# Modulation weights in tiles of their own, multiplied in bursts, in a one-layer diffusion backbone

## The chip, the cores and the metric

The kernel runs on one core of a Trainium2 chip. The time is device time in microseconds (us) of one execution. The kernel before took 2011.56, 2011.78 and 2003.14 us in three runs, a median of 2011.56 us.

The engines named below are TensorE (PE, with PEld for its weight loads), VectorE (DVE), ScalarE (ACT), GpSimd (POOL) and SyncE (SP, which issues the DMAs that this change touches). Each executes its instructions in the order in which they stand in its program, and that order is fixed when the kernel is built.

## The reference, cut to what matters

One trunk layer over 128 context tokens and 256 latent tokens of width 2048. A modulation vector is made of the condition by a product with `w_ada` (2048 x 12288 fp32, 100.7 MB), and is split in six:

```python
mod_ctx = (silu(c_ctx) @ w_ada + b_ada)      # for the context tokens
mod_lat = (silu(c) @ w_ada + b_ada)          # for the latent tokens
shift1, scale1, gate1, shift2, scale2, gate2 = split(mod, 6)
h = rmsnorm(x, pre1) * (1 + scale1) + shift1
proj = h @ w_in                              # gated DeltaNet heads, mLSTM heads, gates
x = x + gate1 * rmsnorm(concat(delta_heads, mlstm_heads) @ w_out, post1)
h = rmsnorm(x, pre2) * (1 + scale2) + shift2
x = x + gate2 * rmsnorm(relu(h @ w1) ** 2 @ w2, post2)
```

The final states of the two kinds of heads are outputs too. All is fp32; `w_in` has 7216 columns, `w1` and `w2` 8192 columns and rows.

## The kernel before, in words

**Large products.** `gemm` (L342) takes a weight matrix by chunks of 256 rows x 512 columns (512 KB). `wchunk` (L321) loads a chunk into a tile `raw` by one DMA on SP's queue (L328), rounds it to `whi` on ScalarE (L332), and takes the rest `wlo = raw - whi` on VectorE (L333). TensorE then makes three products to a pair of tiles (L356 to L358 where the weights are the stationary side and 384 tokens stream, L360 to L362 where the tokens are stationary and 512 weight columns stream): 24 matmuls to a chunk in the first form, 18 in the second.

**The modulation.** `ada_steps` (L172) multiplies `w_ada` by the two condition vectors, spread over 32 columns (`scz`). Each matmul has 32 output rows and goes to one of four column groups of TensorE (`ps[32 * j:32 * j + 32]`), so that four of them stand side by side. In phase 1 a call has two units (the shift1 and the scale1 columns of the same 128 or 256 features); later it has four units of 256 columns. `ada_vec` (L209) does the same sum on VectorE instead, one `scalar_tensor_tensor` (L220) to a row tile and vector, for part of the last two vectors.

**Who decides when.** Both are generators. The list `S.todo` holds them, and after each chunk `gemm` calls `fill` (L235), which hands out steps by a rate: 2.0 steps to a chunk in phase 1, 1.3 in the delta stage, 0.9 in the output projection, 0.3 in the FFN. `drain` (L250) finishes a unit where its result is needed next. A step is one tile of 512 KB: its DMAs (two of 256 KB in phase 1, one later), and its 8 matmuls of 256 columns (or 16 of 128), or in `ada_vec` four VectorE operations. The order of the finished program on each engine is a scheduler's, by these calls and by `high_priority`.

**Buffers.** All loads, of weights and of modulation weights, share one ring: tag `raw` in the pool `wp`, `nraw=5` tiles of 512 KB. `whi` and `wlo` have two tiles each.

**Stages.** In the profiled execution phase 1 (`phase1`, L395: nine pieces of input features, each first modulated by `build_hT`, L288, then multiplied by columns of `w_in`) and the mLSTM heads take roughly the first 320 us, the DeltaNet heads and their output gates go to about 790 us, `mid` (the output projection and the second norm) to about 930 us, and `ffn` and `final` take the rest.

Of the kernel before, what the change touches and what calls it, by code (L numbers as in the profile page):

```python
# [12 lines left out]
F32 = mybir.dt.float32  # L13
# [8 lines left out]
P = 128  # L22
# [148 lines left out]
def ada_steps(S, units, n):  # L171

    nc, c = S.nc, S.c
    nu = len(units)
    npar = 4 // nu
    kn = 1024 // (nu * n)
    ps = S.pa.tile([P, 512], F32, tag="a", name="ps_ada")
    for k in range(0, NK, kn):  # L180
        raw = S.wp.tile([P, kn, nu * n], F32, tag="raw", name="raw_ada", bufs=S.nraw)
        runs = [(0, nu)] if nu == 4 else [(u, u + 1) for u in range(nu)]
        for u, e in runs:
            o = units[u][0] * D + units[u][1]
            nc.sync.dma_start(raw[:, :, u * n:e * n], S.A.w_ada[0, k * P:(k + kn) * P, o:o + (e - u) * n]
                              .rearrange("(k p) n -> p k n", p=P))
        for kk in range(kn):
            for u in range(nu):
                j = u * npar + (k + kk) % npar
                nc.tensor.matmul(ps[32 * j:32 * j + 32, 0:n], lhsT=c.scz[:, k + kk, :],  # L190
                                 rhs=raw[:, kk, u * n:u * n + n], start=k + kk < npar, stop=k + kk >= NK - npar)
        yield
# [11 lines left out]
def ada_vec(S, sec, c0):  # L204

    nc, c = S.nc, S.c
    while S.av is None:
        yield
    acc = S.av.tile([P, 2, 512], F32, tag="adav", name="adav", bufs=1)  # L209
    for kt in range(NK):  # L210
        if kt % 2 == 0:
            raw = S.wp.tile([P, 2, 512], F32, tag="raw", name="raw_av", bufs=S.nraw)
            nc.sync.dma_start(raw, S.A.w_ada[0, kt * P:(kt + 2) * P, sec * D + c0:sec * D + c0 + 512]
                              .rearrange("(k p) n -> p k n", p=P))
        for v in range(2):
            w = c.scz[:, kt, v:v + 1]
            if kt == 0:
                nc.vector.tensor_scalar(acc[:, v, :], raw[:, 0, :], w, None, op0=ALU.mult)
            else:
                nc.vector.scalar_tensor_tensor(acc[:, v, :], in0=raw[:, kt % 2, :], scalar=w, in1=acc[:, v, :],  # L220
                                               op0=ALU.mult, op1=ALU.add)
        if kt % 2:
            yield
# [11 lines left out]
def fill(S, n=None):  # L235

    if n is None:
        S.credit += S.rate
        n = int(S.credit)
        S.credit -= n  # L240
    while n > 0 and S.todo:
        try:
            next(S.todo[0])
            n -= 1
        except StopIteration:
            S.todo.pop(0)
            n -= 1
# [1043 lines left out]
```

## Time and profile before

| what | value |
|---|---|
| timed runs | 2011.56, 2011.78, 2003.14 us |
| the profiled execution | 2004.86 us |
| its span | 2003.1 us |
| PE busy | 1944.5 us, 97% |
| DVE busy | 1166.2 us, 58% |
| ACT busy | 711.1 us, 35% |
| modulation matmuls L190 | 1216 records, 100.6 us busy |
| moved by DMA | 337.25 MB, mean 168 GB/s |

A row of the page's table of groups gives busy time, the mean of one instruction, the idle time of its engine just before it and what ended that. A row of a timeline gives the start in the span, the time, the engine, the line, and in brackets the idle time ahead of it and its releaser. TensorE's rows overlap, since its matmuls are pipelined: the time from one start to the next is what a matmul costs there, not its own length.

### The profile page before, as it was taken

The page shows a single profiled execution, that of the slowest core. Times are in us where ns is not written, and L with a number is a line of the kernel's source. Part 1 is how long each engine was busy: PE and PEld are TensorE (multiplying, and loading weights), DVE is VectorE, ACT ScalarE, POOL GpSimd, SP SyncE. Part 2 cuts the span into 40 slices and gives each one's busy share as a digit, 9 for nine tenths or more (in the row PEclk, how much of TensorE's full clock was granted, in tenths as well). Part 3 has the DMA queues.
Part 4 walks back from the last instruction along what each step waited for, and adds up shares of the span by engine and source line. Part 5 has one row for each costly group of instructions (what it writes and reads, how often), then busy time and mean ns, then how long its engine had stood idle before and what let it go on. Part 6 is the DMA issues. An engine that isn't in the chain of part 4 may idle for free.

```text
span 2003.1 us, 28836 instructions
## 1 busy us (share of the span) xinstructions
PE 1944.5 (97%) x11332; PEld 1673.4 (84%) x11332; DVE 1166.2 (58%) x2144; ACT 711.1 (35%) x1125; POOL 122.8 (6%) x125
## 2 busy tenths in 40 slices
PE   5999997999999999998999999999999999999997
PEld 4677886788888777787998898998989989989886
DVE  3766874668878766767455455556543443343445
ACT  5222243544344334335433342332332423323322
POOL 2000000010000000000100010000000100000002
PEclk9999998999999999998999999999999999999999
DMA  9988438776576566762454554545544344444452
GB/s 271 297 263 261 127 117 167 171 198 192 162 200 188 154 189 201 269 220 64 127 178 158 158 160 147 172 162 158 163 136 130 122 135 126 126 128 127 131 172 105
DMA packets 232356, 337.25 MB, mean 168 GB/s; under 512 B 46272, under 2 KB 115584, under 8 KB 231196
## 3 DMA queue, kind: packets, MB, share of 16 engines
q1 hardware_dynamic: 214120, 333.15, 55.1%
q10 hardware_dynamic: 17620, 2.11, 0.7%
q8 instruction: 89, 1.46, 0.3%
q14 instruction: 47, 0.39, 0.1%
q0 software_dynamic: 480, 0.15, 0.0%
HBM read 326.80 MB, written 8.56 MB: 167 GB/s over the span
## 4 chain that ended last, share of the span: by engine, by line
PE 89%; DMA 5%; DVE 4%; ACT 1%; issue 1%; POOL 0%; SPq 0%; ACTq 0%; DVEq 0%; POOLq 0%
PE ps_g L356 13%; PE ps_g L358 13%; PE ps_g L357 12%; PE ps_dn L360 8%; PE ps_dn L362 8%; PE ps_dn L361 8%; PE ps_g L360 5%; PE ps_g L362 5%; PE ps_g L361 5%; PE ps_ada L190 4%; DMA raw<-w_in 2%; DVE wlo L333 1%; PE ps_o L1027 1%; DMA raw_av<-w_ada 1%; PE ps_num L689 1%
## 5 line engine op out<-in xcount | busy, mean ns | idle before, releaser
L333 DVE TENSOR_TENSOR wlo<-raw,whi 128x1024 fp32r<-128x1024 f32 (+1 forms) x402 | 487.2, 1212 | 568.9 <-ACT whi L332 567.3
L332 ACT CAST whi<-raw 128x1024 fp32r<-128x1024 f32 (+1 forms) x402 | 417.5, 1039 | 1012.3 <-PE ps_g L357 386.8
L356 PE MATMUL ps_g<-h,whi 128*128 128x384 f32 x1536 | 522.8, 340 | 0.6 <-DVE cv L737 0.6
L358 PE MATMUL ps_g<-h,wlo 128*128 128x384 f32 x1536 | 516.3, 337 | 2.1 <-DVE wlo L333 2.1
L357 PE MATMUL ps_g<-h,whi 128*128 128x384 f32 x1536 | 517.0, 337 | 0.0
L356 PEld LDWEIGHTS ps_g<-h,whi 128*128 128x128 f32 x1536 | 288.9, 188 | 20.7 <-issue 18.7
L362 PE MATMUL ps_dn<-wlo,ah 128*128 128x512 f32 x756 | 294.5, 390 | 1.2 <-DVE wlo L333 1.2
L360 PE MATMUL ps_dn<-whi,al 128*128 128x512 f32 x756 | 294.8, 390 | 0.0
L361 PE MATMUL ps_dn<-whi,ah 128*128 128x512 f32 x756 | 294.5, 390 | 0.0
L358 PEld LDWEIGHTS ps_g<-h,wlo 128*128 128x128 f32 x1536 | 288.6, 188 | 5.1 <-DVE wlo L333 3.6
L357 PEld LDWEIGHTS ps_g<-h,whi 128*128 128x128 f32 x1536 | 288.9, 188 | 1.2 <-issue 0.7
L362 PEld LDWEIGHTS ps_dn<-wlo,ah 128*128 128x128 f32 x756 | 141.9, 188 | 31.5 <-DVE wlo L333 2.0
L360 PEld LDWEIGHTS ps_dn<-whi,al 128*128 128x128 f32 x756 | 141.9, 188 | 31.0 <-issue 1.6
L361 PEld LDWEIGHTS ps_dn<-whi,ah 128*128 128x128 f32 x756 | 141.9, 188 | 29.0
L220 DVE SCALAR_TENSOR_TENSOR adav<-raw_av,scz,adav 128x512 f32<-128x512 f32 x180 | 130.4, 773 | 12.3 <-DMA raw_av<-w_ada 12.3
L1148 POOL TENSOR_TENSOR rl<-rl 128x384 f32<-128x384 f32 x64 | 68.0, 1070 | 876.2 <-ACT ah L1147 876.0
L360 PE MATMUL ps_g<-whi,h 128*128 128x512 f32 x288 | 119.1, 413 | 1.3 <-ACT whi L332 1.2
L361 PE MATMUL ps_g<-whi,h 128*128 128x512 f32 x288 | 115.2, 400 | 0.0
L362 PE MATMUL ps_g<-wlo,h 128*128 128x512 f32 x288 | 114.2, 400 | 0.2 <-DVE wlo L333 0.2
L190 PE MATMUL ps_ada<-raw_ada,scz 128*32 128x256 f32 (+1 forms) x1216 | 100.6, 387 | 4.0 <-DMA raw_ada<-w_ada 2.6
L360 PEld LDWEIGHTS ps_g<-whi,h 128*128 128x128 f32 x288 | 54.5, 189 | 24.2 <-issue 11.7
L190 PEld LDWEIGHTS ps_ada<-raw_ada,scz 128*32 128x32 f32 x1216 | 33.9, 113 | 46.4 <-issue 27.2
(400 smaller groups left out, 1895.5 us busy)
## 6 DMA issues: line engine op xcount, KB each, us to landing
raw<-w_ffn SPq DMA_DIRECT2D x256, 512.0 KB, 3.8
raw_ada<-w_ada SPq DMA_DIRECT2D x80, 512.0 KB, 4.8
raw<-w_in SPq DMA_DIRECT2D x74, 512.0 KB, 4.7
raw_ada<-w_ada SPq DMA_DIRECT2D x128, 256.0 KB, 4.5
raw_av<-w_ada SPq DMA_DIRECT2D x48, 512.0 KB, 4.3
raw<-w_in SPq DMA_DIRECT2D x76, 256.0 KB, 3.1
raw<-w_out SPq DMA_DIRECT2D x32, 512.0 KB, 4.5
x<-x_sample SPq DMA_DIRECT2D x2, 1024.0 KB, 10.3
```

The lines of the kernel that those rows point to most:

```text
L190: nc.tensor.matmul(ps[32 * j:32 * j + 32, 0:n], lhsT=c.scz[:, k + kk, :], rhs=raw[:, kk, u * n:u * n + n], start=k + kk < npar, stop=k + k ...
L220: nc.vector.scalar_tensor_tensor(acc[:, v, :], in0=raw[:, kt % 2, :], scalar=w, in1=acc[:, v, :], op0=ALU.mult, op1=ALU.add)
L332: nc.scalar.copy(hi, raw)
L333: nc.vector.tensor_tensor(lo, raw, hi.bitcast(F32), op=ALU.subtract)
L356: nc.tensor.matmul(o, lhsT=hi[:, kk, w], rhs=al, start=st, stop=False)
L357: nc.tensor.matmul(o, lhsT=hi[:, kk, w], rhs=ah, start=False, stop=False)
L358: nc.tensor.matmul(o, lhsT=lo[:, kk, w], rhs=ah, start=False, stop=sp)
L360: nc.tensor.matmul(o, lhsT=al[:, w], rhs=hi[:, kk, :], start=st, stop=False)
L361: nc.tensor.matmul(o, lhsT=ah[:, w], rhs=hi[:, kk, :], start=False, stop=False)
L362: nc.tensor.matmul(o, lhsT=ah[:, w], rhs=lo[:, kk, :], start=False, stop=sp)
L689: nc.tensor.matmul(o, lhsT=l, rhs=r, start=n == 0, stop=n == len(ops) - 1)
L1148: nc.gpsimd.tensor_tensor(rl, rl, rl, op=ALU.mult)
```

## The change: what it does

- `ada_steps` no longer takes tiles of the ring `raw`. In phase 1 it has two tiles of 1 MB, `rawa` (in `wp`) and `rawb` (in `p1`), and after phase 1 `rawa` alone, each with one buffer.
- A step is now a burst: all loads of the burst are issued (in phase 1 2 MB by four DMAs, later 1 MB by one DMA), and then all its matmuls, the last tile and its last row first, so that the first matmul reads what was loaded last. The flags that open and close the sum are counted per column group. A burst has 32 matmuls of 128 columns in the first two units of phase 1, 16 of 256 columns in the others, and 8 of 256 later.
- `yield` gives what the step cost (4 for two tiles, 2 for one), and `fill` takes that from the credit, which may fall below nothing; `drain` ends with a credit of 0.
- `ada_vec` takes 1 MB (four row tiles) into `rawa` by one DMA, and issues the next load right behind the last operation that reads the tile.
- The ring `raw` has 3 tiles (`nraw=3`).

The changed lines stand 9 to 15 lines lower: L190 is L199, the loads L185 are L191, L213 is L222, L220 is L233, L328 is L342, L333 is L347, L360 to L362 are L374 to L376.

```diff
@@ -172,24 +172,33 @@
 
 
 
+
+
     nc, c = S.nc, S.c
     nu = len(units)
     npar = 4 // nu
-    kn = 1024 // (nu * n)
+    kn = 2048 // (nu * n)
     ps = S.pa.tile([P, 512], F32, tag="a", name="ps_ada")
-    for k in range(0, NK, kn):
-        raw = S.wp.tile([P, kn, nu * n], F32, tag="raw", name="raw_ada", bufs=S.nraw)
-        runs = [(0, nu)] if nu == 4 else [(u, u + 1) for u in range(nu)]
-        for u, e in runs:
-            o = units[u][0] * D + units[u][1]
-            nc.sync.dma_start(raw[:, :, u * n:e * n], S.A.w_ada[0, k * P:(k + kn) * P, o:o + (e - u) * n]
-                              .rearrange("(k p) n -> p k n", p=P))
-        for kk in range(kn):
-            for u in range(nu):
-                j = u * npar + (k + kk) % npar
-                nc.tensor.matmul(ps[32 * j:32 * j + 32, 0:n], lhsT=c.scz[:, k + kk, :],
-                                 rhs=raw[:, kk, u * n:u * n + n], start=k + kk < npar, stop=k + kk >= NK - npar)
-        yield
+    runs = [(0, nu)] if nu == 4 else [(u, u + 1) for u in range(nu)]
+    done = [0] * 4
+    kb = kn * len(S.araw)
+    for k0 in range(0, NK, kb):
+        raws = []
+        for (pool, tag), k in zip(S.araw, range(k0, NK, kn)):
+            raw = pool.tile([P, kn, nu * n], F32, tag=tag, name="raw_ada", bufs=1)
+            for u, e in runs:
+                o = units[u][0] * D + units[u][1]
+                nc.sync.dma_start(raw[:, :, u * n:e * n], S.A.w_ada[0, k * P:(k + kn) * P, o:o + (e - u) * n]
+                                  .rearrange("(k p) n -> p k n", p=P))
+            raws.append((k, raw))
+        for k, raw in raws[::-1]:
+            for kk in range(kn)[::-1]:
+                for u in range(nu)[::-1]:
+                    j = u * npar + (k + kk) % npar
+                    done[j] += 1
+                    nc.tensor.matmul(ps[32 * j:32 * j + 32, 0:n], lhsT=c.scz[:, k + kk, :],
+                                     rhs=raw[:, kk, u * n:u * n + n], start=done[j] == 1, stop=done[j] == NK // npar)
+        yield 2 * len(raws)
     t = ada_cols(S, ps, n)
     m = n // P
     if npar == 1:
@@ -205,22 +214,28 @@
 
     nc, c = S.nc, S.c
     while S.av is None:
-        yield
+        yield 1
     acc = S.av.tile([P, 2, 512], F32, tag="adav", name="adav", bufs=1)
+
+    def load(kt):
+        raw = S.wp.tile([P, 4, 512], F32, tag="rawa", name="raw_av", bufs=1)
+        nc.sync.dma_start(raw, S.A.w_ada[0, kt * P:(kt + 4) * P, sec * D + c0:sec * D + c0 + 512]
+                          .rearrange("(k p) n -> p k n", p=P))
+        return raw
+    raw = load(0)
+    yield 1
     for kt in range(NK):
-        if kt % 2 == 0:
-            raw = S.wp.tile([P, 2, 512], F32, tag="raw", name="raw_av", bufs=S.nraw)
-            nc.sync.dma_start(raw, S.A.w_ada[0, kt * P:(kt + 2) * P, sec * D + c0:sec * D + c0 + 512]
-                              .rearrange("(k p) n -> p k n", p=P))
         for v in range(2):
             w = c.scz[:, kt, v:v + 1]
             if kt == 0:
                 nc.vector.tensor_scalar(acc[:, v, :], raw[:, 0, :], w, None, op0=ALU.mult)
             else:
-                nc.vector.scalar_tensor_tensor(acc[:, v, :], in0=raw[:, kt % 2, :], scalar=w, in1=acc[:, v, :],
+                nc.vector.scalar_tensor_tensor(acc[:, v, :], in0=raw[:, kt % 4, :], scalar=w, in1=acc[:, v, :],
                                                op0=ALU.mult, op1=ALU.add)
+        if kt % 4 == 3 and kt < NK - 1:
+            raw = load(kt + 1)
         if kt % 2:
-            yield
+            yield 1
     ps = S.pa.tile([P, 512], F32, tag="a", name="ps_av")
     for j in range(4):
         nc.tensor.matmul(ps[32 * j:32 * j + 32, 0:256], lhsT=c.ones[:, 0:32], rhs=acc[:, j % 2, 256 * (j // 2):][:, 0:256],
@@ -234,22 +249,21 @@
 
 def fill(S, n=None):
 
-    if n is None:
-        S.credit += S.rate
-        n = int(S.credit)
-        S.credit -= n
-    while n > 0 and S.todo:
+
+    S.credit += S.rate if n is None else n
+    while S.credit >= 1 and S.todo:
         try:
-            next(S.todo[0])
-            n -= 1
+            S.credit -= next(S.todo[0])
         except StopIteration:
             S.todo.pop(0)
-            n -= 1
+            S.credit -= 1
 
 
 def drain(S, left):
     while len(S.todo) > left:
-        fill(S, 1)
+        S.credit = 1
+        fill(S, 0)
+    S.credit = 0.0
 
 
 def ada_later(S, sec, nvec=0):
@@ -263,7 +277,7 @@
 
 def gate_step(S, i):
     gate_rows(S, i)
-    yield
+    yield 1
 
 
 def gate_rows(S, i):
@@ -405,6 +419,7 @@
     NP = len(pieces)
     S.todo = [ada_steps(S, [(0, P * k), (1, P * k)], P * kn) for k, kn in pieces]
     S.rate = 2.0
+    S.araw = [(S.wp, "rawa"), (p1, "rawb")]
 
     for p, (k0, kn) in enumerate(pieces):
         if p == 0:
@@ -1207,7 +1222,7 @@
 def body(tc, A, O):
     with ExitStack() as ctx:
         nc = tc.nc
-        S = SimpleNamespace(nc=nc, tc=tc, A=A, O=O, todo=[], credit=0.0, rate=1.7, nraw=5, av=None)
+        S = SimpleNamespace(nc=nc, tc=tc, A=A, O=O, todo=[], credit=0.0, rate=1.7, nraw=3, av=None)
         ent = ctx.enter_context
         sub = lambda st, nm, bufs=1: st.enter_context(tc.tile_pool(name=nm, bufs=bufs, reuse_waits="tile"))
         S.cp = ent(tc.tile_pool(name="cp", bufs=1))
@@ -1236,6 +1251,7 @@
                 S.ml = sub(ms, "ml", 2)
                 for h in range(HB):
                     mlstm_head(S, h)
+            S.araw = [(S.wp, "rawa")]
             S.da = sub(mx, "da", 2)
             S.dl = sub(mx, "dl", 2)
             S.de = sub(mx, "de", 2)
```

Three places of the order of the instructions follow. A row names the line, the operation, what it writes and reads, and the size; "x4" is four alike in a row.

SP in phase 1, at the first units of 256 columns, before (`raw_ada` are modulation weights, `raw` weights of `w_in`):

```order
L328 DMA raw<-w_in 128x2x512
L185 DMA raw_ada<-w_ada 128x2x256 x4
L328 DMA raw<-w_in 128x2x512
L185 DMA raw_ada<-w_ada 128x2x256 x4
L328 DMA raw<-w_in 128x2x512
L185 DMA raw_ada<-w_ada 128x2x256 x4
```

The same place now, with the semaphores for which an instruction waits (PE is a wait for matmuls, DVE for the operations that end the use of a `raw` tile, DMAHW for an earlier DMA):

```order
L342 DMA raw<-w_in 128x2x512 [waits DMAHW6_49,DVE_49]
L342 DMA raw<-w_in 128x2x512 [waits DMAHW7_49,DVE_49]
L191 DMA raw_ada<-w_ada 128x4x256 [waits DMAHW4_49,DMAHW3_49,PE_49]
L191 DMA raw_ada<-w_ada 128x4x256 [waits DMAHW1_49,DMAHW2_49,DMAHW0_49,PE_49]
L191 DMA raw_ada<-w_ada 128x4x256 x2
L342 DMA raw<-w_in 128x2x512 [waits DVE_49]
L342 DMA raw<-w_in 128x2x512 [waits DMAHW5_49,DVE_49]
```

Four loads of 512 KB now stand together, the first of them waits for TensorE, and the loads of `w_in` stand behind them.

TensorE in phase 1, in the products with tokens stationary, before (`ps_ada` is the modulation, `ps_g` the product with `w_in`):

```order
L190 MATMUL ps_ada<-raw_ada,scz 32x256 x4
L360 MATMUL ps_g<-whi,h_171 128x512
L361 MATMUL ps_g<-whi,h_170 128x512
L362 MATMUL ps_g<-wlo,h_170 128x512
L165 MATMUL ps_col<-ident,modrow 128x128 x2
L360 MATMUL ps_g<-whi,h_171 128x512
```

And now:

```order
L199 MATMUL ps_ada<-raw_ada,scz 32x256 x16
L376 MATMUL ps_g<-wlo,h_170 128x512
L374 MATMUL ps_g<-whi,h_171 128x512
L375 MATMUL ps_g<-whi,h_170 128x512
L165 MATMUL ps_col<-ident,modrow 128x128 x2
L376 MATMUL ps_g<-wlo,h_170 128x512
```

Runs of 1 to 8 modulation matmuls became runs of 16; over the whole program the number of such runs falls from 119 to 67.

VectorE at the end of `mid`, where the second norm is made, before (L1113 adds the residual, L310 makes the matrix `diag` for which TensorE waits):

```order
L1113 SCALAR_TENSOR_TENSOR x_1_8124<-x_1_8124,r1r,xr_8129 128x1024
L1081 TENSOR_TENSOR x_2_8125<-ps_g,gp_1_8127 128x512
L1108 TENSOR_REDUCE s_9144<-ssm 128x1
L1118 TENSOR_REDUCE s_9154<-ss_9123 128x1
L282 TENSOR_SCALAR r1v<-s_9144 128x1
L282 TENSOR_SCALAR r20v<-s_9154 128x1
L1113 SCALAR_TENSOR_TENSOR x_2_8125<-x_2_8125,r1r,xr_8130 128x1024 x2
L310 TENSOR_SCALAR diag<-ident,r20r 128x128
```

And now:

```order
L1128 SCALAR_TENSOR_TENSOR x_1_7976<-x_1_7976,r1r,xr_7981 128x1024
L1123 TENSOR_REDUCE s_8955<-ssm 128x1
L1133 TENSOR_REDUCE s_8965<-ss_8934 128x1
L233 SCALAR_TENSOR_TENSOR adav<-raw_av,scz,adav 128x512
L296 TENSOR_SCALAR r1v<-s_8955 128x1
L296 TENSOR_SCALAR r20v<-s_8965 128x1
L233 SCALAR_TENSOR_TENSOR adav<-raw_av,scz,adav 128x512
L1128 SCALAR_TENSOR_TENSOR x_2_7977<-x_2_7977,r1r,xr_7982 128x1024 x2
L324 TENSOR_SCALAR diag<-ident,r20r 128x128
L1133 TENSOR_REDUCE s_8973<-ss_8934 128x1
L233 SCALAR_TENSOR_TENSOR adav<-raw_av,scz,adav 128x512
L296 TENSOR_SCALAR r21v<-s_8973 128x1
```

Operations of `ada_vec` (`adav`) now stand among the steps of the norm, where there was none.

## Rows read from the trace of the kernel before

**Rows 1.** The page's first part: busy us, share of the span, instructions.
```profile
PE 1944.5 (97%) x11332; PEld 1673.4 (84%) x11332; DVE 1166.2 (58%) x2144; ACT 711.1 (35%) x1125; POOL 122.8 (6%) x125
```

**Rows 2.** Windows: stretch, length, busy PE, PEld, DVE, ACT, POOL, PEclk, DMA share, GB/s.
```profile
0.00:320.00 320.00, 298.61 (x1853) 233.33 (x1854) 212.01 (x440) 104.60 (x146) 14.44 (x27) 0.98 0.72 219
320.00:790.00 470.00, 454.99 (x3466) 370.19 (x3466) 328.27 (x949) 204.32 (x470) 21.20 (x16) 0.99 0.66 181
```

**Rows 3.** Windows of the same stretches, modulation matmuls L190 alone: PE, PEld.
```profile
0.00:320.00 320.00, 44.14 (x600) 17.69 (x600) 0.98 0.72 219
320.00:790.00 470.00, 55.85 (x608) 16.05 (x608) 0.99 0.66 181
```

**Rows 4.** Waits of PE: what waited, for what, us in total, times, longest.
```profile
PE ps_hT L295 <- DVE s L1118: 7.2, 1, 7.2
...
PE ps_ada L190 <- DMA raw_ada<-w_ada: 2.6, 1, 2.6
```

**Rows 5.** Timeline of PE around two runs of modulation matmuls in phase 1.
```profile
157.71 0.39 PE L361 MATMUL ps_g<-whi,h 128*128 128x512 f32 x1
157.94 0.39 PE L362 MATMUL ps_g<-wlo,h 128*128 128x512 f32 x1
158.25 1.07 PE L190 MATMUL ps_ada<-raw_ada,scz 128*32 128x256 f32 x16
159.25 0.50 PE L360 MATMUL ps_g<-whi,h 128*128 128x512 f32 x1
159.59 0.40 PE L361 MATMUL ps_g<-whi,h 128*128 128x512 f32 x1
...
38.37 0.40 PE L361 MATMUL ps_g<-whi,h 128*128 128x512 f32 x1
38.69 0.64 PE L190 MATMUL ps_ada<-raw_ada,scz 128*32 128x256 f32 x8
39.26 0.50 PE L362 MATMUL ps_g<-wlo,h 128*128 128x512 f32 x1
39.60 0.40 PE L360 MATMUL ps_g<-whi,h 128*128 128x512 f32 x1
```

**Rows 6.** DMA issues, 205 to 260 us: count, KB each, median us to landing.
```profile
raw<-w_in SPq DMA_DIRECT2D x13, 512.0 KB, 3.7
```

**Rows 7.** DMA issues of the whole span.
```profile
raw_ada<-w_ada SPq DMA_DIRECT2D x80, 512.0 KB, 4.8
...
gp<-gpd SPq DMA_DIRECT2D x2, 1024.0 KB, 8.0
```

**Rows 8.** Windows, columns as in rows 2: a light, a dense and a long stretch.
```profile
205.00:260.00 55.00, 55.00 (x275) 48.55 (x275) 46.26 (x72) 15.79 (x19) 0.00 (x0) 1.00 0.42 121
60.00:80.00 20.00, 19.32 (x130) 12.90 (x129) 16.62 (x35) 6.17 (x10) 0.00 (x0) 1.00 0.98 321
60.00:200.00 140.00, 139.09 (x910) 102.86 (x909) 96.79 (x173) 33.07 (x41) 0.00 (x0) 1.00 0.85 272
```

**Rows 9.** Timeline of PE near the start, around the second unit of modulation.
```profile
27.48 2.77 PE L190 MATMUL ps_ada<-raw_ada,scz 128*32 128x128 f32 x42 [1.31 <-DVE modcol L167]
30.18 0.59 PE L435 MATMUL ps_gates<-h,wgh 128*96 128x384 f32 x2
```

**Rows 10.** Windows around the second norm.
```profile
914.00:916.00 2.00, 0.00 (x0) 0.00 (x0) 1.00 (x6) 1.15 (x2) 0.70 (x2) 0.56 0.98 363
924.00:926.00 2.00, 2.00 (x15) 2.00 (x15) 1.89 (x5) 0.60 (x2) 0.00 (x0) 0.88 0.00 0
```

**Rows 11.** Timeline of DVE, then PE, at the end of the second norm.
```profile
918.27 0.28 DVE L310 TENSOR_SCALAR diag<-ident,r20r 128x128 f32<-128x128 f32 x1
...
918.61 0.80 PE L295 MATMUL ps_hT<-diag,x 128*128 128x128 f32 x2 [7.22 <-DVE s L1118]
```

**Rows 12.** Timeline of DVE in the FFN, one chunk with modulation work.
```profile
1147.04 1.23 DVE L333 TENSOR_TENSOR wlo<-raw,whi 128x1024 fp32r<-128x1024 f32 x1 [2.94 <-ACT whi L332]
1148.18 2.73 DVE L220 SCALAR_TENSOR_TENSOR adav<-raw_av,scz,adav 128x512 f32<-128x512 f32 x4
1151.20 1.23 DVE L333 TENSOR_TENSOR wlo<-raw,whi 128x1024 fp32r<-128x1024 f32 x1 [0.29 <-ACT whi L332]
```

## The prediction, made before the changed kernel ran

> **What bounds the kernel now.** I read the page's first part first, then windows by stage, the waits of TensorE, the windows of the modulation matmuls alone, and last timelines around single runs of them. TensorE is busy 97% of the span and the next engine 58% [rows 1]. In phase 1 and the delta stage it is busy 298.6 of 320 and 455.0 of 470 us [rows 2], so what it spends on the modulation, 44.1 and 55.9 us [rows 3], lies on the path, and a wait of TensorE put there lies on it too. The whole span has one wait of it for a modulation load, 2.6 us [rows 4]: the shared ring of five tiles lets these loads run ahead. The longest wait near the change is 7.2 us before the second norm's transposes [rows 4]. The change touches three things: the number of runs of modulation matmuls, when their loads may start, and where VectorE's share stands.
>
> **Fewer runs: -15.5 us.** A run costs more than its matmuls, because TensorE changes from full to 32-column work and back. Around a run of 8 matmuls (16 records) the starts go from 157.94 to 159.59, 1.65 us [rows 5]; five matmuls before it are 0.23 apart, of which two lie in this stretch (the one at 157.94 and the one at 159.25), so the run costs 1.65 - 0.46 = 1.19. A run of 4 costs 39.60 - 38.37 less two such, 1.23 - 0.46 = 0.77 [rows 5]. The difference gives 0.42 for four matmuls, 0.107 each, and leaves 0.77 - 0.43 = 0.34 us fixed to a run. By this rule (half for 128 columns) the 119 runs of before cost about 102 us, and the trace has 44.1 + 55.9 = 100 [rows 3], so the rule holds over the whole. Now there are 67 runs (order of the program): 52 x 0.34 = 17.7 us less. Before's first four runs stood in TensorE's idle start, where saving them is worth nothing, about 2.2 us: -15.5. If only the runs of 4 in the dense parts pay in full it may be -12; if the longer weight loads at a change (0.50 against 0.39 a matmul [rows 5]) are more than I count, -18.
>
> **The loads now wait for the burst before them.** Each tile has one buffer. By the order, the first load of a burst waits on SP for the last matmul of the burst before; nothing is loaded ahead of that. So each burst starts no sooner than one whole load after the last. How long is that? A lone load of 512 KB lands 3.7 us after its issue [rows 6], in a stretch with 121 GB/s [rows 8]. A dense stretch of 20 us moves 321 GB/s at a DMA share of 0.98 [rows 8], so the bytes take 1.6 us and 2.1 are fixed. 2 MB: 2.1 + 2.097/0.321 = 2.1 + 6.5 = 8.6 us. 1 MB: 2.1 + 3.3 = 5.4; the rows of 1 MB show 8.0 [rows 7], but those are broadcast reads.
> Against that stands the work between two bursts in TensorE's order. In phase 1 I counted the matmuls between bursts and took 0.2285 us for one of 512 columns and 0.1735 for one of 384 (pitch in long runs): between two bursts stand for instance 31 products and two transposes, 7.4 us. The 14 gaps behind the first full burst are 7.3, 5.9, 8.7, 6.8, 7.8, 7.5, 7.7, 8.5, 7.5, 7.5, 8.2, 7.3, 7.7 and 8.1 us, the sum of what 8.6 exceeds them by is 14 us. Take +14; with 7.0 us for a load it is 1, with 9.8 (the 272 GB/s of the long stretch [rows 8]: 2.1 + 7.7) 31. In the delta stage the 40 bursts have gaps of 4.7 to 22 us, eight of them of 5.0 and about ten more up to 5.7, where one chunk (24 x 0.1735 = 4.2 us) stands between. With 5.4 the sum is 4, with 5.7 8: take +6; at 5.0 it is 0.6, at 6.0 13.
> The weight loads behind the waiting instruction on SP are late too: by TensorE's time between bursts at most two chunks, and those of the ring's 3 tiles cover about two chunks of 4.1 us. I cost this at nothing, since whi and wlo of the next chunk are made ahead; if the cover is gone, `whi` waits 1 us in each of the 14 bursts, and that is in the upper end. Three tiles where nothing else is loaded: a lone load of 3.7 us within a chunk of 4.16 leaves two chunks of lead, nothing.
>
> A rule bears on the load. The Trainium skill ("DMA: Bandwidth & Descriptors", "Anatomy of one DMA") gives a DMA about 2.0 us fixed, and the rest by 436 GB/s. That makes an estimate of 3.2 us for 512 KB, where the trace has 3.7 [rows 6], and 6.8 for 2 MB, at which the waits of phase 1 would be about 1 us. The trace's rates are 321 over 20 us [rows 8] and 363 in 2 us [rows 10], and the sum goes by the first, which holds for longer than one load.
>
> **The start: +1 us.** Before, the second unit's matmuls stand ahead of the gates' product, 2.77 us of modulation until 30.18 [rows 9], and TensorE was at work through a time in which it now waits for the gate weights: now its first unit is one burst of 32, and the second comes after the first products. The clock may fall in such a wait; at the second norm 7.2 us of idle time bring it to 0.56 of full, and it is still at 0.88 some 6 us after the restart [rows 10], which is what it could cost here (up to 4 us). The 2 us of taking the second unit's matmuls off the start go the other way. Range -2 to +4, I take +1.
>
> **The second norm: +3 us.** Here VectorE is a chain of single steps, TensorE idles 7.2 us for it [rows 11]. In the order now, `adav` operations stand in it: two before the first `diag`, two before the second, and more behind. Each takes 0.68 us (2.73 for four [rows 12]), so 2 x 0.68 = 1.4 before TensorE starts and about as much again among the first transposes: +3. If their load is late the chain waits for it too (up to +6); if VectorE had the time while it waits for GpSimd's rstd, 0.
>
> **The FFN: +1 us.** Four operations to a chunk fit before: 1.23 + 2.73 = 3.96 us within the chunk's 4.16, with 0.29 idle left [rows 12]. They are the same number now, 1 MB tiles make them stand in groups of 16 at the starts of some products; the lead of the ring takes that. A group whose load is late makes `wlo` late behind it: -1 to +6, I take +1.
>
> **The sum.** From the profiled execution of 2004.9 us: -15.5, +14, +6, +1, +3, +1 = +9.5, which gives 2014.4. Two of the timed runs lie near 2011.6, 7 us above the profiled execution, and one at 2003.1. I stay with the sum, 2014 us.
>
> **Rivals.**
> *The loads land within the gaps.* If 2 MB land in 7.0 and 1 MB in 5.0 us, waits are 1 + 1 us instead of 20: 2004.9 - 15.5 + 1 + 1 + 1 + 3 + 1 = 1996 us, faster. For it: TensorE's gaps of 7.3 to 8.7 us fit such loads, 363 GB/s occurs [rows 10], with which 2 MB take 7.9, and SP has fewer DMAs to issue. Against: over a load's length 321 GB/s is the densest that I found, and the weight loads share it.
> *The loads queue, and the waits outweigh the saving.* One mechanism: a burst's load starts only when the last burst has ended, then it stands in the same 16 DMA engines with the weights. Phase 1 was dense before, share 0.85 and 272 GB/s over 140 us [rows 8], and modulation loads of only 512 KB took 4.8 us [rows 7]. At that rate 2 MB take 9.8 and 1 MB 6.0: 31 + 13 us, and the later stages 6 + 3: 2004.9 - 15.5 + 1 + 31 + 13 + 6 + 3 = 2043 us, slower. It decides from the landing time at which the waits reach the -10.5 of everything else, about 7.9 us for 2 MB; 9 us make it measurable. Against it: between bursts TensorE uses only 512 KB in 4.1 us, 128 GB/s, so the rest of the rate is free.
> *The bursts bring no saving.* If a change of column groups costs by matmuls, not by runs, the 17.7 us don't exist and the waits do: 2004.9 + 1 + 14 + 6 + 3 + 1 = 2030 us. For it: only two lengths of runs gave the 0.34. Against: the rule's total meets the trace.
>
> **How the numbers follow.** My forecast, the waits eat the saving, 0.40 (its own range 2003 to 2024); loads within the gaps 0.27; waits outweigh 0.23; no saving 0.10. What a measurement tells from no change is 0.5%, 10 us, so faster is under 2001.5 and slower over 2021.6. Faster: 0.8 of the first rival and a tenth of the forecast, 0.26. Slower: nearly all of the two last, and a tenth of the forecast, 0.35. The same: 0.39. The range goes from the first rival's 1993 (its waits gone, the runs at -18) to 2040, which leaves out half of the queueing case.
>
> **What would show it.** Right: modulation matmuls at about 84 us instead of 100.6, waits of TensorE for `raw_ada` of about 20 us in some 30 places, landing of the 2 MB bursts near 8.6 us, two `adav` before the first `diag`. Wrong: waits under 5 us (first rival), or landing near 10 us and over 40 us of waits (second), or modulation matmuls still near 100 us (third). A wait of TensorE for `whi` or `wlo` behind the bursts would say that the ring of three, which I cost at nothing, is too short.

## The result: 2061.62 us, slower by 2.7%

The changed kernel took 2060.94 to 2068.07 us in four runs, median 2061.62, against 2011.61 before: a ratio of 1.0267 (95% interval 1.0249 to 1.0285). The forecast was 2014, the range ended at 2040. The profiled execution took 2068.07 us, its span is 2066.3, which is 63.2 above the span of before. Of these 63 some 13 us lie between executions of one kernel, since the profiled one is the slowest of four here and one of the faster ones before (2004.86 us); a stage's share below carries some of that.

The page's first part for the changed kernel answers to [rows 1]:

```profile
PE 1946.6 (94%) x11332; PEld 1697.5 (82%) x11332; DVE 1167.7 (57%) x2144; ACT 712.9 (35%) x1125; POOL 127.3 (6%) x125
```

TensorE is busy as long as before (1944.5), and idle for 61 us more (2066.3 - 1946.6 against 2003.1 - 1944.5). Two things cancel in the busy time. The windows of the modulation matmuls alone (PE, PEld, clock, DMA share, GB/s) answer to [rows 3]:

```profile
0.00:320.00 320.00, 34.17 (x600) 18.96 (x604) 0.97 0.69 215
320.00:790.00 470.00, 48.04 (x624) 16.27 (x616) 0.95 0.65 176
```

They fell by 17.8 us, from 100.0 to 82.2, as forecast (84); all other matmuls together grew by some 20, at a lower granted clock (0.95 against 0.99 in the second stretch). The waits of TensorE (what waited, for what, us in total, times, longest), which answer to [rows 4]:

```profile
PE ps_ada L199 <- DMA raw_ada<-w_ada: 42.1, 22, 6.9
PE ps_hT L309 <- DVE s L1133: 9.5, 2, 9.0
PE ps_g L372 <- DVE wlo L347: 9.3, 9, 2.2
...
PE ps_g L376 <- DVE wlo L347: 7.2, 4, 3.7
PE ps_cn L689 <- DVE ks L687: 6.8, 1, 6.8
PE ps_gates L450 <- DVE h L318: 6.4, 3, 4.1
```

The wait for modulation loads went from 2.6 us in one place to 42.1 in 22, twice my 20: 15.8 in phase 1 (14 places), 21.9 between 320 and 460 us (six), 4.4 behind that (two). Where does the time go? The starts of the same matmul of the large products (the first, the second, and so on, line by line) in two traces give the lag of one behind the other, at the end of each stage. The last column is the forecast's sum by stage: the -15.5 of the runs shared out by the runs saved there (23 in phase 1, the rest later), with the waits and the other terms.

| up to (us, before) | work that ends there | lag of the changed kernel | forecast |
|---|---|---|---|
| 238 | phase 1, to its last quarter | +11.3 | +9 |
| 457 | mLSTM heads, overlapped with the first delta products | +45.0 | } +6 |
| 793 | delta heads, gates | +41.3 | } |
| 943 | output projection, second norm | +58.5 | +9 |
| 1982 | FFN | +63.1 | +10 |

Phase 1 came out near what was worked out; three kernels below whose edit doesn't touch phase 1 have +9.3 to +13.6 there, which shows how far one stage varies from one trace to the next. 34 us arise in the mLSTM heads, for which the forecast has nothing, and 17 in the output projection and the norm, where it has 3.

In the heads, this is TensorE's timeline around one burst (start, us, engine, line, operation; in brackets the idle time ahead and its releaser), with SP's issues of the same time:

```profile
403.07 1.07 PE L199 MATMUL ps_ada<-raw_ada,scz 128*32 128x256 f32 x16
...
416.36 1.93 PE L199 MATMUL ps_ada<-raw_ada,scz 128*32 128x256 f32 x16 [6.95 <-DMA raw_ada<-w_ada]
418.23 0.69 PE L372 MATMUL ps_g<-h,wlo 128*128 128x384 f32 x1
418.72 0.52 PE L370 MATMUL ps_g<-h,whi 128*128 128x384 f32 x1
```

```profile
400.81 0.36 SPq L692 DMA_DIRECT2D out_C<-cf  x1
401.21 0.42 SPq L693 DMA_DIRECT2D out_n<-cf  x1
401.73 0.92 SPq L342 DMA_DIRECT2D raw<-w_in  x2
404.20 0.37 SPq L191 DMA_DIRECT2D raw_ada<-w_ada  x1
410.40 0.37 SPq L342 DMA_DIRECT2D raw<-w_in  x1
```

The load is issued as soon as the burst of 403.07 has ended, as the order had said (`SPq` is SP issuing a DMA). But it takes from 404.20 to 416.36 to reach TensorE, 12.2 us where I had put 5.4. The burst behind the wait takes 1.93 instead of 1.07 us, and the products after it start 0.32 to 0.5 apart instead of 0.17: the clock has fallen to its lower level, 1.2 GHz, in the 7 us without a matmul (granted share 1.00 ahead of them, 0.50 from 417 to 420 us), and is back at 1.00 from 425 us on. The windows (length, PE, PEld, DVE, ACT, POOL, granted clock, DMA share, GB/s) show this, and in the first two what moves in those 12 us:

```profile
404.00:411.00 7.00, 5.42 (x34) 4.80 (x30) 5.31 (x16) 5.42 (x13) 0.85 (x1) 1.00 0.50 28
411.00:415.00 4.00, 0.00 (x0) 0.00 (x0) 1.21 (x4) 0.40 (x2) 0.00 (x0) 0.67 0.89 312
417.00:420.00 3.00, 3.00 (x21) 2.00 (x11) 0.00 (x0) 0.00 (x0) 0.00 (x0) 0.50 0.21 37
425.00:428.00 3.00, 3.00 (x28) 2.02 (x27) 1.83 (x9) 1.99 (x4) 0.00 (x0) 1.00 0.76 35
```

For 7 us the DMA engines are half busy and move 28 GB/s, then 312 GB/s, more than 1 MB in 4 us. So the load isn't long, it is held up. Ahead of it in SP's queue stand two loads of weights, and ahead of these the stores of one head's final state, of which `out_n` is 128 elements of 4 bytes, one in each partition. That is a suspicion at this point, and the experiments take it up.

In the output projection, VectorE's timeline at the second price:

```profile
924.63 3.40 DVE L233 SCALAR_TENSOR_TENSOR adav<-raw_av,scz,adav 128x512 f32<-128x512 f32 x5 [2.91 <-DMA raw_av<-w_ada]
927.95 1.22 DVE L347 TENSOR_TENSOR wlo<-raw,whi 128x1024 fp32r<-128x1024 f32 x1
```

and TensorE's, which waits for that `wlo`:

```profile
929.23 0.80 PE L376 MATMUL ps_g<-wlo,y 128*128 128x512 f32 x1 [3.73 <-DVE wlo L347]
```

`wlo` stands behind five `adav` operations, and these wait for their load. At the norm, TensorE's wait grew from 7.22 [rows 11] to 8.99 us, and its first transposes stand 2.2 us apart, with `adav` operations between the steps that release them:

```profile
975.27 1.65 PE L309 MATMUL ps_hT<-diag,x 128*128 128x128 f32 x6 [8.99 <-DVE s L1133]
977.43 1.65 PE L309 MATMUL ps_hT<-diag,x 128*128 128x128 f32 x6 [0.52 <-DVE s L1133]
979.60 1.65 PE L309 MATMUL ps_hT<-diag,x 128*128 128x128 f32 x6 [0.52 <-DVE diag L324]
```

Over the span the `scalar_tensor_tensor` operations of VectorE wait 45.0 us for `raw_av` (12.3 before).

### The profile page after: what moved, and what is told of

Its sections match the earlier page's. It is cut to its first block, busy times and chain, and to the rows that moved or that the text cites. A ratio compares the mean times of both kernels' runs of the same rounds, so it can differ in the third digit from the quotient of the medians.

```text
span 2066.3 us, 28612 instructions
## 1 busy us (share of the span) xinstructions
PE 1946.6 (94%) x11332; PEld 1697.5 (82%) x11332; DVE 1167.7 (57%) x2144; ACT 712.9 (35%) x1125; POOL 127.3 (6%) x125
## 4 chain that ended last, share of the span: by engine, by line
PE 77%; DMA 14%; DVE 5%; issue 1%; ACT 1%; SPq 1%; POOL 0%; DVEq 0%; ACTq 0%; POOLq 0%
PE ps_g L372 11%; PE ps_g L370 11%; PE ps_g L371 11%; DMA raw_ada<-w_ada 9%; PE ps_dn L376 8%; PE ps_dn L374 8%; PE ps_dn L375 8%; PE ps_ada L199 3%; PE ps_g L374 3%; PE ps_g L376 3%; PE ps_g L375 3%; DMA raw_av<-w_ada 3%; DVE wlo L347 1%; DVE adav L233 1%; DMA raw<-w_in 1%
## 5 line engine op out<-in xcount | busy, mean ns | idle before, releaser
L347 DVE TENSOR_TENSOR wlo<-raw,whi 128x1024 fp32r<-128x1024 f32 (+1 forms) x402 | 487.4, 1213 | 566.9 <-ACT whi L346 561.8
L372 PE MATMUL ps_g<-h,wlo 128*128 128x384 f32 x1536 | 523.9, 342 | 9.3 <-DVE wlo L347 9.3
L372 PEld LDWEIGHTS ps_g<-h,wlo 128*128 128x128 f32 x1536 | 292.8, 191 | 17.9 <-DVE wlo L347 13.0
L370 PEld LDWEIGHTS ps_g<-h,whi 128*128 128x128 f32 x1536 | 293.1, 191 | 15.4 <-issue 10.5
L371 PEld LDWEIGHTS ps_g<-h,whi 128*128 128x128 f32 x1536 | 293.2, 191 | 3.8 <-issue 3.1
L376 PE MATMUL ps_dn<-wlo,ah 128*128 128x512 f32 x756 | 294.3, 389 | 0.0
L374 PE MATMUL ps_dn<-whi,al 128*128 128x512 f32 x756 | 294.2, 389 | 0.0
L376 PEld LDWEIGHTS ps_dn<-wlo,ah 128*128 128x128 f32 x756 | 141.9, 188 | 30.0 <-DVE wlo L347 0.4
L374 PEld LDWEIGHTS ps_dn<-whi,al 128*128 128x128 f32 x756 | 141.9, 188 | 29.6 <-issue 0.4
L233 DVE SCALAR_TENSOR_TENSOR adav<-raw_av,scz,adav 128x512 f32<-128x512 f32 x180 | 127.8, 756 | 45.0 <-DMA raw_av<-w_ada 45.0
L199 PE MATMUL ps_ada<-raw_ada,scz 128*32 128x256 f32 (+1 forms) x1216 | 82.2, 394 | 42.2 <-DMA raw_ada<-w_ada 42.1
L374 PE MATMUL ps_g<-whi,h 128*128 128x512 f32 x288 | 117.3, 407 | 0.0
L376 PE MATMUL ps_g<-wlo,h 128*128 128x512 f32 x288 | 115.6, 401 | 0.0
L199 PEld LDWEIGHTS ps_ada<-raw_ada,scz 128*32 128x32 f32 x1216 | 35.2, 115 | 74.0 <-DMA raw_ada<-w_ada 40.3
L376 PE MATMUL ps_g<-wlo,y 128*128 128x512 f32 x180 | 73.7, 409 | 7.3 <-DVE wlo L347 7.2
```

The costliest lines, as they stand in the source:

```text
L347: nc.vector.tensor_tensor(lo, raw, hi.bitcast(F32), op=ALU.subtract)
L370: nc.tensor.matmul(o, lhsT=hi[:, kk, w], rhs=al, start=st, stop=False)
L371: nc.tensor.matmul(o, lhsT=hi[:, kk, w], rhs=ah, start=False, stop=False)
L372: nc.tensor.matmul(o, lhsT=lo[:, kk, w], rhs=ah, start=False, stop=sp)
L374: nc.tensor.matmul(o, lhsT=al[:, w], rhs=hi[:, kk, :], start=st, stop=False)
L376: nc.tensor.matmul(o, lhsT=ah[:, w], rhs=lo[:, kk, :], start=False, stop=sp)
```

## The experiments

All times are medians, ratios are to the kernel before on the same chip. Except where it is said, every kernel starts from the changed one. "n stores" are the eight stores of the mLSTM state n. The code is cut to the lines on which an experiment turns, and its comments are added here. In every kernel with `rawa0` and `rawa1` each 1 MB tile has become two of 512 KB, with one load each, for `ada_vec` too.

**Loads ahead after phase 1 (later_turn).** `rawa` is split in two halves that take turns in `ada_steps`; `ada_vec` loads both halves behind its eighth operation, as before.

```diff
-S.araw = [(S.wp, "rawa")]
+S.araw = [[(S.wp, "rawa0")], [(S.wp, "rawa1")]]   # a burst takes the next group
```

> The changed kernel (2061.6 us), but the 1 MB of rawa is two tiles of 512 KB, and after phase 1 a burst of ada_steps takes one of them in turn (4 matmuls), so that one load is always under way while the other tile is multiplied. Phase 1 bursts (2 MB) and the pace of ada_vec (1 MB at a time) are as in the changed kernel. Theory A, the load after phase 1 starts only when the burst before it has ended and lands after 10 to 12 us in the mLSTM heads, where TensorE idles and its clock falls: the lag of 36 us that arises between 360 and 430 us goes, 23 more runs cost 23 x 0.34 = 8 us, so about 2034 us; TensorE's wait for raw_ada falls from 42 to about 17 us, all of it in phase 1. Theory B, the ring of three weight tiles is too short: the waits for whi and wlo stay and the lag too, the runs cost 8 us more, about 2070 us.

2056.54 us, 1.0221 (1.0198 to 1.0244): 5 us better. Theory A asked for 28, and TensorE's wait for `raw_ada` is 43.2, as long as before. B has the waits for `whi` and `wlo` stay, and they fell from about 20 to 11. Neither holds. By stage, the heads cost 43 us here (lag +18.5 to +61.9) instead of 34, phase 1 7 more, and the gain stands behind 793 us, where the lag grows by 4 instead of 22. That a lead of one load of 512 KB isn't enough where a load comes 7 us late is argued from the 18.4 us of waits for `raw_ada` that stay between 238 and 460 us; the lateness itself had to be found.

**One load ahead for ada_vec (vec_turn).**

```diff
-raw = S.wp.tile([P, 4, 512], F32, tag="rawa", ...)         # next load after the 8th operation
+raw = S.wp.tile([P, 2, 512], F32, tag=f"rawa{kt // 2 % 2}", ...)   # two in turn
```

> The changed kernel, but rawa is two tiles of 512 KB, and ada_vec takes them in turn, each loaded again behind the last operation that reads it; ada_steps is as in the changed kernel, a burst of both tiles. Theory A: VectorE waits 45 us for raw_av in the changed kernel, with wlo queued behind, and the lag of 14 us between 900 and 925 us (and 5 in the FFN) comes of that: about 2047 us, and VectorE's wait for raw_av falls from 45 to about 12 us. Theory B, ring too short or the place of the adav operations in the norm alone: 2055 to 2062 us, with the wait of TensorE for wlo near 929 us as before.

2061.49 us, 1.026 (1.0224 to 1.0295), the time of the changed kernel. VectorE's wait for `raw_av` fell from 45.0 to 15.2 us, near A's 12. The lag between 793 and 890 us, which grows by 13 us in the changed kernel, grows by -2 here (+50.1 to +48.5), and from 943 us to the end by 0.2 instead of 5, so A's mechanism is borne out in these stages. But the heads cost 41 us in this kernel instead of 34 and phase 1 4 more, for which I have no cause, and the total lies in B's span: it doesn't show the gain, the stages do.

**Loads ahead in phase 1 (p1_turn).**

```diff
-S.araw = [(S.wp, "rawa"), (p1, "rawb")]
+S.araw = [[(S.wp, "rawa0"), (S.wp, "rawa1")], [(p1, "rawb0"), (p1, "rawb1")]]
```

> The changed kernel, but in phase 1 a burst is 1 MB (8 matmuls of 256 columns), and the pair of halves in wp and the pair in p1 take turns, so that one burst's load is under way while the other is multiplied; after phase 1 as in the changed kernel. Theory A: 14 more runs (and 8 where the pair is split by the scheduler) cost 5 to 8 us, the waits of some 14 us behind the first full burst go: about 2054 us. Theory B: the waits in phase 1 are the rate of the DMA engines and stay: 2066 us.

2041.9 us, 1.0158 (1.0139 to 1.0178): 20 us better. In the first 320 us the wait for `raw_ada` goes from 15.8 us (14 places) to 2.7, and the lag at 238 us from +11.3 to -1.8, which is 13.1 and nearly the 14 that the forecast had worked out for these waits. The rest came in the output projection, and I hadn't expected it: a half of `rawa` comes free ahead of the other, VectorE's wait for `raw_av` is 15.1 us, and the 13 us there are gone too (+28.6 to +27.2 between 793 and 890).

**The n stores out of the heads (n_late).**

```diff
-nc.sync.dma_start(S.O.n[0, 0, d, h].rearrange("(p o) -> p o", o=1), cf[:, DVB:DVB + 1])
+nc.scalar.copy(S.nn[:, 4 * d + h:4 * d + h + 1], cf[:, DVB:DVB + 1])
...
+nc.tensor.transpose(ps[0:8, 0:P], S.nn, S.c.ident)          # once, before the FFN
+nc.vector.tensor_copy(g[0:8], ps[0:8, 0:P])
+nc.sync.dma_start(O.n[0, 0].rearrange("d h p -> (d h) p"), g[0:8])
```

> The changed kernel, but the eight stores of the mLSTM state n (128 elements of 4 bytes each, one behind each head's store of C) are not issued in the heads; the columns are kept, transposed on TensorE before the FFN and stored by rows of 512 bytes in one DMA. Theory A with the stores as the reason for the slow loads: loads of 1 MB in the mLSTM heads land in about 6 us instead of 10 to 12, TensorE's wait for raw_ada there falls from 18.6 us (395, 416, 438 and 449 us) to under 6, and half of the 36 us goes: about 2040 us. Rival: the 4-byte stores are not the reason (the loads of the gates bo, the 1 KB rows of w_in or the state loads are): 2061 us, the same waits.

2019.25 us, 1.004 (1.0026 to 1.0053): 42 of the 50 us are gone, twice what I expected. TensorE's waits between 320 and 460 us in the changed kernel and then here:

```profile
PE ps_ada L199 <- DMA raw_ada<-w_ada: 21.9, 6, 6.9
PE ps_cn L689 <- DVE ks L687: 6.8, 1, 6.8
PE ps_g L370 <- ACT whi L346: 3.0, 1, 3.0
...
```

```profile
PE ps_ada L199 <- DMA raw_ada<-w_ada: 1.9, 2, 1.7
```

And the windows of that stretch, columns as above, of the changed kernel and of n_late:

```profile
320.00:460.00 140.00, 107.46 (x622) 87.96 (x614) 61.85 (x199) 49.65 (x120) 6.74 (x9) 0.85 0.75 157
```

```profile
320.00:460.00 140.00, 137.79 (x925) 116.33 (x924) 97.43 (x295) 70.87 (x156) 7.83 (x9) 1.00 0.75 239
```

At the same DMA share of 0.75 the engines move 239 instead of 157 GB/s, and the clock stays at its upper level, since TensorE no longer waits. The DMA issues of the stretch, first with the stores, then without (count, KB, median us to landing):

```profile
raw_ada<-w_ada SPq DMA_DIRECT2D x11, 1024.0 KB, 7.2
raw<-w_in SPq DMA_DIRECT2D x18, 256.0 KB, 4.6
raw<-w_in SPq DMA_DIRECT2D x4, 512.0 KB, 9.9
gb<-gbd SPq DMA_DIRECT2D x9, 128.0 KB, 7.1
```

```profile
raw_ada<-w_ada SPq DMA_DIRECT2D x18, 1024.0 KB, 4.9
raw<-w_in SPq DMA_DIRECT2D x28, 256.0 KB, 4.9
raw<-w_in SPq DMA_DIRECT2D x8, 512.0 KB, 4.3
gb<-gbd SPq DMA_DIRECT2D x7, 128.0 KB, 2.3
```

Loads of three kinds land sooner, not those of the modulation alone; the median of the 256 KB loads of weights doesn't move.

**Is it the store, or the tile that it holds? (n_split).** The column is copied out of `cf` as in n_late, and stored by 4-byte elements from the copy.

```diff
+nc.scalar.copy(S.nn[:, 4 * d + h:4 * d + h + 1], cf[:, DVB:DVB + 1])
+nc.sync.dma_start(S.O.n[0, 0, d, h].rearrange("(p o) -> p o", o=1), S.nn[:, 4 * d + h:4 * d + h + 1])
```

> The changed kernel (2061.6 us); the column n is copied out of cf into a tile of its own, as in n_late (2019 us), but is still stored from there in each head by 128 elements of 4 bytes, so that cf is free without that store and the DMA engines still have it. Theory A, the 4-byte stores slow what is behind them in the DMA engines: 2055 to 2065 us, loads of modulation weights still 10 us late in the mLSTM heads. Rival D, what n_late removed was the wait for the tile cf (a store holds it): 2019 to 2025 us.

2070.09 us, 1.0278 (1.0259 to 1.0296), 5 over A's span and far from D's. The stretch has 28.3 us of waits for `raw_ada` in five places. D falls: what costs is the store itself, whatever tile it reads. The single DMA packets in the traces show where. In SP's queue a packet of 1 KB takes 0.046 us and one of 4 KB 0.159 (medians between 320 and 460 us). Packets of that queue of 512 bytes and more that took over 1.5 us number 196 in the changed kernel (the longest 7.9 us) and 206 in n_split, of which 191 and 194 start within 12 us of the issue of an n store; n_late has four in its whole span, of at most 2.1 us.

**The kernel before without the n stores (before_n_late).** The same edit as n_late, on the kernel before.

> The kernel before (2011.6 us) with the eight 4-byte-element stores of the mLSTM state n taken out of the heads in the way of n_late. Theory A (the stores slow what stands behind them in the DMA engines): the ring's lead hides slow loads in the kernel before, but its three waits for cf (10.9 us, the tile from which n is stored) and the half clock after them go: 1994 to 2000 us, and against n_late (2019 us) the change then costs about 20 us instead of 50. Rival (the stores are slow only for loads without lead): 2008 to 2014 us, no change.

1992.34 us, 0.989 (0.9876 to 0.9905). The kernel before paid 20 us for these stores, and the changed one 42; that the ring's lead hid the other half is argued. The long packets fall from 150 to 9. In the kernel before TensorE also waited 10.9 us in three places for `cf`, the tile that n is stored from, and no longer does; n_split wasn't tried on that kernel, so how its 20 us divide between the held tile and late loads is open. Without the stores the change still costs 2019.25 - 1992.34 = 27 us.

**Both causes (p1_turn_n).** p1_turn and n_late together.

> p1_turn (bursts of 1 MB in phase 1 from two pairs of halves in turn; 2042 us) and n_late (2019 us) together. If the waits of phase 1 for want of a load ahead and the slow loads behind the n stores are two causes that add: 2061.6 - 20 - 42 = 2000 us. If p1_turn's 20 us came from what n_late also removes: 2015 us or over.

1997.08 us, 0.9914 (0.9896 to 0.9931): they add. Lag at 238 us -2.0, at 457 -8.8, at the end -10.5; the 27 us that the change costs without the n stores are 5 here, so 22 of them were loads without lead. By the lags of n_late and of this kernel 11 of them lie in phase 1, 12 in the output projection and the norm (by the split halves) and 5 in the FFN, and the heads give 7 back.

**Bursts alone, from the shared ring (ring_burst, ring_burst_n).** The ring of five and `ada_vec` as before; a burst takes two of its tiles. The second kernel has the n stores out of the heads.

```diff
-S.araw = [(S.wp, "rawa"), (p1, "rawb")]
+S.araw = [[(S.wp, "raw"), (S.wp, "raw")]]     # bufs=S.nraw, nraw=5
```

> The kernel before with its ring of five tiles of 512 KB for all loads and its ada_vec, and of the change only the bursts: ada_steps takes two tiles of the ring, issues both loads and multiplies both, the last first, and the step counts 2. 80 runs of modulation matmuls instead of 119. Theory A (a run costs 0.34 us, and loads with the ring's lead land in time): 39 x 0.34 = 13 us less, about 1998 us, with waits of TensorE for raw_ada under 6 us. Rival (runs cost nothing, or bursts alone bring the waits): 2011 us or over.

2036.36 us, 1.0106 (1.0089 to 1.0123). The modulation matmuls take 85.6 us, 15 less than before, and the whole is 23 us longer: A's saving is there and A's time is wrong. Between 300 and 470 us TensorE waits 15.4 us for `raw_ada`.

> ring_burst (2036 us: shared ring of five, bursts of two of its tiles) with the n stores taken out of the heads. Theory A, bursts need the DMA engines free of the n stores, since a burst takes two of the ring's tiles and shortens its lead: the lag of 50 us that ring_burst builds up between 300 and 350 us goes, 1985 to 1995 us, against 1992.3 without bursts. Rival: bursts from the ring starve the weights everywhere, 2005 us or over.

2005.4 us, 0.996 (0.9946 to 0.9975), 13 over before_n_late, which has no bursts: the rival's number, and not A's. The lag is +7.4 at 238 us and +15.2 at 457, where before_n_late has -0.7 and -17.1. That two of five tiles at a time take the lead from the weights fits the waits for `whi` in 7 places (4.5 us), but these are too few to settle it, and it stays argued.

**Is it the adav operations in the norm? (n_late_vec).** From n_late; the last vector's units depend on the norm.

```diff
+nc.vector.tensor_scalar(z, r2[2], 0.0, None, op0=ALU.mult)
+nc.vector.tensor_scalar(S.scb, c.scz[:, :, 0:2], z, None, op0=ALU.add)
-w = c.scz[:, kt, v:v + 1]
+w = (c.scz if S.scb is None else S.scb)[:, kt, v:v + 1]
```

> n_late (2019 us), and the units of ada_vec for the last vector read a copy of the condition that is made from the second norm's last rstd (plus 0 times it), so that their operations can't be put ahead of the end of the norm's chain. In VectorE's order no adav operation stands in the norm any more. Theory C, these operations in the chain and the half clock behind the longer wait cost 10 us: about 2009 us, TensorE's waits for diag at the norm (15.0 us in n_late) under 8 with the 7.2 us of the kernel before in all. Rival: they stand in gaps of VectorE and cost nothing, 2019 us.

2020.3 us, 1.0038 (1.0023 to 1.0053), the same as n_late: the rival's number, though not for the rival's reason. The norm did get shorter: the lag at 943 us is +1.5 instead of +5.9. By 991 us it is +7.5 against +6.9. The operations moved to the FFN's first chunks and hold up a `wlo` there (1.94 us at 980).

**All loads in turn (all_turn_n, all_turn_late).** p1_turn_n with later_turn and vec_turn; then also the norm's edit.

> p1_turn_n (1997 us) with halves of rawa in turn after phase 1 too, for ada_steps (bursts of 4, one load ahead) and for ada_vec. TensorE's waits for raw_ada in p1_turn_n are 6.4 us in all, so there is little left to win: the 17 more runs cost 17 x 0.34 = 6 us, 1997 to 2003 us. Rival: the delta stage's loads without lead still cost more than they show, 1985 to 1992 us.

1990.22 us, 0.988 (0.986 to 0.9901). The time lies in the rival's span, 7 us under p1_turn_n, but the two profiled spans are alike (1992.3 and 1992.6) and the intervals overlap. Whether the delta heads' loads without lead still cost something isn't told apart here.

> all_turn_n (1990.2 us), and the units of ada_vec for the last vector read a copy of the condition that is made behind the second norm (as in n_late_vec), so that none of their operations stands in the norm's chain. In all_turn_n the norm and the FFN's first chunks lose about 6 us against the kernel before. Theory C, with two halves in turn no wlo stands behind a late load at the start of the FFN, so that the gain of the norm is kept: 1984 us. Rival: what the norm gains is lost again at the start of the FFN, as in n_late_vec: 1988 to 1993 us.

1988.05 us, 0.9895 (0.9877 to 0.9913), the lower edge of the rival's span: at 943 us the lag is -17.7 against -11.9 in all_turn_n, at the end -13.9 against -10.8, so about half of the norm's gain is lost again; the two times themselves overlap in their intervals.

These two and before_n_late are 1.0 to 1.2% faster than the kernel before, p1_turn_n 0.9%; the intervals of the three overlap, so none is best. In that company the bursts win nothing: all_turn_n has 87.3 us of modulation matmuls, before_n_late 99.9, and the spans are 1992.3 and 1991.8.

## Why the prediction was wrong, step by step

- **What bounds the kernel: right.** TensorE's stalls go into the time one for one, and more (below).
- **Fewer runs, -15.5: right as a cost of TensorE.** 82.2 us against the 84 forecast. As a gain of time it never showed by itself; in all_turn_n and before_n_late 12.6 us of it turn into waits elsewhere.
- **"The loads now wait", phase 1, +14: right in size, in part by luck.** 15.8 us in 14 places, of which 2.4 at the start; p1_turn takes 13.1 off that stage. The landing was composed otherwise than I worked out. Two bursts in TensorE's timeline, and the issues of SP between them:

```profile
80.51 1.93 PE L199 MATMUL ps_ada<-raw_ada,scz 128*32 128x256 f32 x32 [0.91 <-DMA raw_ada<-w_ada]
...
91.36 1.93 PE L199 MATMUL ps_ada<-raw_ada,scz 128*32 128x256 f32 x32 [1.05 <-DMA raw_ada<-w_ada]
```

```profile
81.64 2.33 SPq L191 DMA_DIRECT2D raw_ada<-w_ada  x4
```

From the first issue to the burst this cycle takes 9.7 us (8.8 to 10.2 in the 14 of them), of which the four issues are 2.33, for which I had nothing. But the first issue comes 0.8 us ahead of the end of the burst before (80.51 + 1.93 = 82.44), when the half of that burst which reads its tile is over. From burst to burst that leaves 8.9, near my 8.6: two errors nearly cancelled, and so far the number was luck.
- **"The loads now wait", after phase 1, +6: the step that failed.** I took 1 MB to land in 5.4 us everywhere, from a stretch with weights alone. Behind the heads that was fair: 4.4 us of waits in two places. In the mLSTM heads it was not: one load took 12.2 us, and TensorE's waits there are 21.9. Rows of the trace of before spoke against it, and I used none: between 320 and 460 us its 512 KB loads `raw_ada` land after 7.3 us, its 128 KB loads `cn` after 9.7 and its 128 KB stores `out_C` after 8.7, and TensorE's largest wait for a tile of the heads is this:

```profile
PE ps_num L689 <- ACT cf L676: 10.9, 3, 7.4
```

A load issued with no lead inherits whatever stands ahead of it in the DMA engines, here the n stores. That was 34 us of lag there, and n_late turns it into -14. The half clock after waits of 4 to 7 us is part of it, and I hadn't priced it: 0.85 over 140 us.
- **"I cost this at nothing", the ring of three.** TensorE's waits for `whi` and `wlo` rose from 6.1 us to about 20, mostly where `wlo` stands behind an `adav` (10 of 13 places). They fell to 11 in later_turn with the ring still of three tiles; a longer ring beside the bursts' own tiles was not tried, so what its length costs is open.
- **The second norm, +3: too small for the stage, fair for the norm.** From 793 to 943 us the lag grew by 17. Some 13 (up to 890 us) belong to the output projection, where the loads of `ada_vec` go one at a time through SP behind blocked weight loads, and VectorE waits with `wlo` behind it. vec_turn and p1_turn take them away. About 4 are the norm's own; n_late_vec moves them into the FFN, and by the traces all_turn_late keeps about half of that gain.
- **The start, +1: met, as far as the trace tells.** The lag is 1.6 us at 20 us and again 1.6 at 70. The 2.2 us that I took off for the start's four runs are 1.4 at 0.34 each, which changes nothing.
- **The FFN, +1: measured +5.** VectorE's wait for `raw_av` is 30.5 us between 980 and 1990 us; in vec_turn it is 5.6, and the lag grows by 0.2 there.
- **The rivals.** The one that ended slower had the right sign and the wrong price: the mechanism "a burst's load starts only when the last burst has ended, then stands in the same engines" is what happened, and its signs came (landing near 10 us, over 40 us of waits), but the engines were held up behind small stores, not full (0.50 busy at 28 GB/s). Its 2043 us lie 19 short. The bursts do bring their saving (82.2 us), so the last rival is out, and by 42.1 us of waits the loads didn't land within the gaps. The Trainium skill's rule ("DMA: Bandwidth & Descriptors", "Anatomy of one DMA") is a fit for one DMA issued by GpSimd, by which 2 MB land in an estimated 6.8 us. The trace doesn't show that for the whole way of a burst's four loads, which SP issues (9.7); the rule's 436 GB/s for the bytes alone is nearly met, as the next section's row shows.

## What to carry to other kernels

Where a change takes the lead from a load, its landing time is no longer a property of the load but of everything that is ahead of it in the queue, so read the slowest landings of each stage, not the median of the quiet one. A tile with one buffer and a whole burst between two loads makes the longest of them visible; two halves in turn keep the same memory and most of the gain (p1_turn); behind the n stores they did not (later_turn). And look for stores of single 4-byte elements: turning eight columns with one transpose was worth 1.1% in the kernel before, more than the 17.7 us that the fewer runs could win.

## What the hardware showed that I had not expected

A store of 128 elements of 4 bytes, 0.5 KB in all, holds up what is issued behind it: 7 us at 28 GB/s with the DMA engines half busy, and 17 single packets of 1 to 4 KB that start between 402.5 and 411 us take 1.5 to 7.9 us. That these stores do it is shown (n_late, n_split); why a packet behind them takes so long is open, and so is whether it is the size of the elements or their number, since no kernel stored the same column there in larger pieces. The eight loads of the state n, of the same shape, don't do it: n_late still issues them in the heads, from 310 to 350 us, and its first packet of over 1.5 us comes after 480. Once the way is free the engines are faster than I had seen. The rate in 40 slices of 404 to 417 us of the changed kernel:

```profile
GB/s 76 35 0 50 44 25 35 32 25 25 9 28 41 19 16 22 22 41 9 25 0 44 72 145 268 287 265 359 432 416 432 413 419 384 284 214 148 117 22 0
```

413 to 432 GB/s in five slices, 1.6 us, against the 321 over 20 us by which I had worked.
